# Storing keys and values unsplit, and splitting them in attention

## The chip, the cores and the metric

The kernel runs on one core of a Trainium2 chip. The metric is the device time of one execution in microseconds, as a median of several runs. A core has five engines that run side by side, each from its own queue in order: TensorE (PE in the profile, with PEld for its weight loads), VectorE (DVE), ScalarE (ACT), GpSimd (POOL) and SyncE (SP). SP issues nearly all DMAs of this kernel.

## The reference

One step of a two-layer decoder trunk over 512 prompt rows and 8 x 4 sample rows, 544 rows in all, with 1024 channels. Layer A ends with a projection to shared keys, values and log-forget values; layer B begins with a feed-forward block (FFN) and then attends to them.

```python
def shared_kv(h, kv_norm, w_kvf, b_f, k_norm):
    xs = rmsnorm(h, kv_norm)
    kvf = xs @ w_kvf
    k = rmsnorm(kvf[..., :D_ATT].reshape(bsz, L, N_HEADS, HEAD_DIM), k_norm)
    v = kvf[..., D_ATT:2 * D_ATT].reshape(bsz, L, N_HEADS, HEAD_DIM)
    logf = jax.nn.log_sigmoid((kvf[..., 2 * D_ATT:] + b_f).astype(jnp.float32))
...
# layer B
h = h + 0.5 * swiglu(rmsnorm(h, ffn1_norm[i]), ffn1_w1[i], ffn1_w3[i], ffn1_w2[i])
q = rmsnorm((rmsnorm(h, mix_norm[i]) @ att_w_q[j]).reshape(bsz, L, N_HEADS, HEAD_DIM), q_norm[j])
# per head, for blocks of 128 queries
s = q k^T * scale + csum_q - csum_k          # csum: running sum of logf, causal mask
o = softmax(s) @ v
```

k, v, logf are outputs too. The sample rows attend to pages of a cache in the same way.

## The kernel before

Activations lie transposed: channels on the 128 partitions, the 544 rows on the free axis. Products run in a form of float32 (fp32r) that keeps part of the mantissa, so every factor is split into a high part `hi` (a cast, on ScalarE) and a low part `lo = x - hi` (a subtraction, on VectorE), and a product is three matmuls: hi·hi, hi·lo, lo·hi. `split_pair` (L279, L280) does this for activations, `_split` (L192, L193) for 128x1024 blocks of weights, which stream in by DMA (L159).

SBUF buffers of 4352 bytes a partition are called `big` (44 of them), those of half the size `tmp` (8). PSUM has three buffers `ps` of two banks and two `pb` of one.

The order of each engine's queue is set by the framework's scheduler, which replays the program as written with a model of times and gives every engine a fixed order; only the body of an FFN is in the order of its code. An engine that waits at one instruction holds back everything behind it in its queue.

The places that matter here, in order of time:

- *Projection of shared keys and values* (`kv`). First a tile for the log-forget values, whose further work (`forget`, L801 to L886) runs in the background, on VectorE up to L817, then as a running sum over 512 positions on POOL (nine steps L827) that ends in the cast L836 on ScalarE. Then eight tiles for the heads' keys, then eight for the values, each 48 matmuls into a `ps` buffer. In the values' loop, per head: VectorE scales the value tile (L755); the key of the same head is normalized (`k_norm`, L774), written out, split, and its pair written to `kd` in DRAM; the values of the head before are turned by TensorE (`v_turn`, five transposes L786 and L787 into a `ps` buffer), split from PSUM, their sample rows copied by ScalarE (L791), and the pair written to `vd`. One input of the next FFN is scaled and split (`prep`, L291, L292).
- *Forms for the next FFN.* The FFN multiplies 2x2 blocks by a scheme with seven products, which takes sums and differences of its inputs. `forms` (L301 to L308 and two pairs of splits) makes them for two channel chunks at a time: four sets for the eight chunks. `kv` makes two of them, after heads 3 and 5; `more` in `ffn` makes those that are missing between the four plain tiles at the FFN's start (copied out at L417).
- *FFN body.* The seven products of a block come in the order 1 5 6 2 7 3 4, each into PSUM (L480), with three accumulators in turn, two of them in `ps`. Product 6 goes where 1 was, 7 where 6 was, 4 where 7 was, each after the copy L488 or the sum L497 has emptied it.
- *Attention.* The order of its steps is written by hand in `ORDER`: `f` fetches a head's keys and values, `a` makes its scores, L1011 to L1017 are the softmax, `t` turns the probabilities, `v` multiplies by the values. The scheduler interleaves the steps of neighbouring heads.

Of the kernel before, what the change touches and what calls it, by code (L numbers as in the profile page):

```python
# [22 lines left out]
F32 = mybir.dt.float32  # L23
F32R = mybir.dt.float32r
I32 = mybir.dt.int32
AF = mybir.ActivationFunctionType
ALU = mybir.AluOpType
AX = mybir.AxisListType

P = 128  # L30
D = 1024
NC_ = D // P
SEQ = 512
# [7 lines left out]
NH = 8  # L41
# [42 lines left out]
def whole(p):  # L84

    return p[:].rearrange("p a b -> p (a b)")[:, 512 - CUT:512 - CUT + T]


class Builder:
# [469 lines left out]
    def gmlp(self, h, box, on_chunk):  # L559
# [78 lines left out]
        u_tile(2)  # L638
        assert self.chain is None
        v_turn(0)  # L640
        v_turn(1)
        for c, spatials, turns in ((3, (0,), (2, 3)), (4, (1,), (4,)), (5, (2, 3), (5,)), (6, (4, 5), (6, 7)),
                                   (7, (6, 7), ())):
            u_tile(c)
            for k in turns:
                v_turn(k)
            for k in spatials:
                spatial(k)
# [72 lines left out]
    def kv(self, h, box, ffn_gain):  # L721

        nc, o = self.nc, self.o
        xs = self.pairs(box)
        p, rstd = self.tile_rstd(xs, box["acc"])
        f = self.big()[:, 0, :]
        self.evac(lambda p=p: nc.vector.tensor_tensor(f, whole(p), rstd, ALU.mult))
        self.bg.append(self.forget(f))
        kraw = []
        self.kd = self.dram.tile([NH, P, 2, SEQ], F32, name="kd")  # L730
        self.vd = self.dram.tile([NH, P, 2, SEQ], F32, name="vd")
        self.vsd = self.dram.tile([NS, D], F32, name="vsd")
        sqs, bcs, rows = [], [], {}
        for hh in range(NH):
            p = self.tile_mm(xs)
            if hh % 2 == 0:
                kt = self.big()

            def take(p=p, kc=kt[:, hh % 2, :]):
                nc.vector.tensor_tensor(kc, whole(p), rstd, ALU.mult)  # L740
                kraw.append(kc)
                sqs.append(self.square(kc))
            self.evac(take)
            if hh == 5:
                bcs += self.head_rows(sqs[:4])
            if hh >= 6:
                rows[hh - 6] = bcs[hh - 6]()
        vpend = None
        nxt = {"x": {}, "f": []}
        for hh in range(NH):  # L750
            p = self.tile_mm(xs)
            if hh == 0:
                bcs += self.head_rows(sqs[4:])
            vc = self.tmp()
            last = nc.vector.tensor_tensor(vc, whole(p), rstd, ALU.mult)  # L755
            nc.sync.dma_start(out=o["v"][hh], in_=vc)
            if vpend is not None:
                self.v_turn(*vpend)
            vpend = (hh, vc)
            with self.tc.issue_after(last.ins):  # L760
                self.k_norm(hh, kraw, rows)
            if hh + 2 < NH:
                rows[hh + 2] = bcs[hh + 2]()
            nxt["x"][hh] = self.prep(h[hh], ffn_gain + hh)
            if hh in (3, 5):
                nxt["f"].append(self.forms(h, ffn_gain, len(nxt["f"]), self.pairs(nxt)))
        self.v_turn(*vpend)
        return nxt, rstd

    def k_norm(self, hh, kraw, rows):  # L770
        nc = self.nc
        bc = rows.pop(hh)
        kn = kraw[hh]
        nc.vector.scalar_tensor_tensor(kn, kn, self.gain(G_K), bc, ALU.mult, ALU.mult)  # L774
        nc.sync.dma_start(out=self.o["k"][hh], in_=kn)
        nc.gpsimd.tensor_copy(self.ks[:, hh, :], kn[:, SEQ:])
        pair = self.big(F32R)
        self.split_pair(pair, kn[:, :SEQ], slice(0, SEQ))
        nc.sync.dma_start(out=self.kd[hh], in_=pair[:, :, :SEQ].bitcast(F32))

    def v_turn(self, hh, vc):

        nc = self.nc
        t = self.ps()
        for j in range(4):
            nc.tensor.transpose(t[:, 0, j * P:(j + 1) * P], vc[:, j * P:(j + 1) * P], self.ident)  # L786
        nc.tensor.transpose(t[:NS, 1, :P], vc[:, SEQ:], self.ident)  # L787
        pair = self.big(F32R)
        self.split_pair(pair, t[:, 0, :], slice(0, SEQ))
        vs = self.small.tile([P, P], F32, tag="vs", name=self.name("vs"), bufs=2)  # L790
        nc.scalar.copy(vs[:NS, :P], t[:NS, 1, :P])  # L791
        nc.sync.dma_start(out=self.vd[hh], in_=pair[:, :, :SEQ].bitcast(F32))
        nc.sync.dma_start(out=self.vsd[:, hh * P:(hh + 1) * P], in_=vs[:NS, :P])

    def forget(self, x):
# [173 lines left out]
    def attention(self, xs, acc, h_out, on_chunk):  # L969
        nc = self.nc  # L970
# [3 lines left out]
        st = {}  # L974
        W = (256, 256, 384, 512)

        def fetch(h):
            kp, vp = self.big(F32R), self.big(F32R)
            nc.sync.dma_start(out=kp[:, :, :SEQ].bitcast(F32), in_=self.kd[h])
            nc.sync.dma_start(out=vp[:, :, :SEQ].bitcast(F32), in_=self.vd[h])  # L980
            st["kv", h] = (kp, vp)

        def prep_q(h):
            st["q", h] = self.big(F32R)
# [2 lines left out]
        def qk(h):  # L987
            kp, _ = st["kv", h]
            qp = st.pop(("q", h))
            S = [self.ps(), self.ps()]  # L990
            r0 = 32 * (h % 4)
            for i in range(4):
                out = S[i // 2][:, i % 2, :]
                w, qs = W[i], slice(i * P, (i + 1) * P)
                nc.tensor.matmul(out[:, :w], self.L[r0:r0 + 32, h // 4, qs], self.R[r0:r0 + 32, 0, :w],  # L995
                                 start=True, stop=False)
                nc.tensor.matmul(out[:, :w], qp[:, 0, qs], kp[:, 0, :w], start=False, stop=False)  # L997
                nc.tensor.matmul(out[:, :w], qp[:, 0, qs], kp[:, 1, :w], start=False, stop=False)
                nc.tensor.matmul(out[:, :w], qp[:, 1, qs], kp[:, 0, :w], start=False, stop=False)
                if i == 0:  # L1000
                    nc.tensor.matmul(out[:, :256], self.identr, self.neg[:, 128:384], start=False, stop=True)
                else:
                    nc.tensor.matmul(out[:, (i - 1) * P:(i + 1) * P], self.identr, self.neg[:, 0:256],
                                     start=False, stop=True)
            ps = []
            for i in range(4):
                w = (i + 1) * P
                sc = S[i // 2][:, i % 2, :w]
                m, l = self.sm(1), self.sm(1)
                p = self.tmp()  # L1010
                nc.vector.tensor_reduce(m, sc, AX.X, ALU.max, negate=True)  # L1011
                nc.scalar.activation(p[:, :w], sc, AF.Exp, bias=m, accum_out=l)
                nc.vector.reciprocal(l, l)
                if i in (1, 2):
                    nc.gpsimd.tensor_scalar(p[:, :w], p[:, :w], l, None, ALU.mult)
                else:
                    nc.scalar.activation(p[:, :w], p[:, :w], AF.Copy, scale=l)  # L1017
                ps.append(p)
            st["p", h] = ps
# [17 lines left out]
        def pv(h):  # L1037
            pt = st.pop(("t", h))
            _, vp = st.pop(("kv", h))
            mv = ((pt[0], 0, 512), (pt[1], 0, 384), (pt[2], 0, 256), (pt[2], 256, 256))  # L1040
            acc = self.pb()
            for j, (t3, c0, n) in enumerate(mv):
                vs = slice(j * P, (j + 1) * P)
                out = acc[:, 512 - n:512]
                nc.tensor.matmul(out, vp[:, 0, vs], t3[:, 0, c0:c0 + n], start=j == 0, stop=False)
                nc.tensor.matmul(out, vp[:, 0, vs], t3[:, 1, c0:c0 + n], start=False, stop=False)
                nc.tensor.matmul(out, vp[:, 1, vs], t3[:, 0, c0:c0 + n], start=False, stop=j == 3)
            o[h] = self.big(F32R)
            self.split_pair(o[h], acc, slice(0, SEQ))

# [114 lines left out]
        def project(c):  # L1165
# [5 lines left out]
            on_chunk(c, slice(HT, T))  # L1171

        do = dict(q=tile, s=stat, n=norm, f=fetch, p=prep_q, a=qk, t=turn, v=pv, K=self.load_k, V=self.load_v,
                  z=sample_q, S=sample_qk, T=sample_turn, P=sample_pv, O=sample_out, x=load_vs, h=project_half,
                  o=project)
# [215 lines left out]
```

## Time and profile before

| what | us |
|---|---|
| three runs, median (lowest, highest) | 2083.34 (2082.64, 2084.26) |
| the profiled execution's own time | 2082.28 |
| its span | 2080.5 |
| TensorE busy in the span | 2052.7 |
| VectorE, ScalarE, POOL busy | 1509.0, 940.0, 180.5 |

The span is the time from the first to the last recorded instruction; the execution's own time is 1.8 us longer. In the rows of the profile an instruction is named by line, engine, operation and `out<-in`, and the brackets or the arrow name what ended the idle time ahead of it.

### The profile page before, as it was taken

Reading aid. Unit: us, or ns where it says so; the run is one execution under the profiler, and the core shown is the slowest. Engines: PE = TensorE matmul, PEld = TensorE weight load, DVE = VectorE, ACT = ScalarE, POOL = GpSimd, SP = SyncE. Lnnn points to the kernel's source line nnn. Section 1 sums busy time; section 2 is a strip of 40 time slices with the busy share of each in tenths; the row PEclk is TensorE's granted clock in tenths of the full one; section 3 lists DMA queues with packets and bytes.
Section 4 is the critical chain, followed back from the end, with each engine's and each line's share of the span. In section 5 each row is a group of like instructions: output and inputs, shape, how many; then the busy total and the mean of one; then the engine's idle time right before and its main releaser. Section 6 shows DMA issues by size and latency. Waiting matters only on the chain.

```text
span 2080.5 us, 38809 instructions
## 1 busy us (share of the span) xinstructions
PE 2052.7 (99%) x16388; PEld 2016.0 (97%) x16388; DVE 1509.0 (73%) x1874; ACT 940.0 (45%) x1389; POOL 180.5 (9%) x226
## 2 busy tenths in 40 slices
PE   8999999999999999999999999999999999999999
PEld 8999999999999999999999999999977999999999
DVE  7877777456687878776688777786465797777773
ACT  6534344323554434454355443444364654343451
POOL 0000000300100000052140000002041300000020
PEclk9999999999999999999999999999999999999999
DMA  5223234212223233422193222326467332322321
GB/s 183 90 96 119 72 102 154 83 44 82 86 88 112 78 106 99 136 92 88 62 351 109 99 102 92 112 87 200 150 201 260 102 102 72 112 91 93 126 98 44
DMA packets 93776, 237.94 MB, mean 114 GB/s; under 512 B 9490, under 2 KB 27442, under 8 KB 93602
## 3 DMA queue, kind: packets, MB, share of 16 engines
q1 hardware_dynamic: 93458, 235.42, 33.9%
q8 instruction: 129, 2.11, 0.4%
q14 instruction: 45, 0.37, 0.1%
q10 hardware_dynamic: 144, 0.04, 0.0%
HBM read 218.94 MB, written 16.49 MB: 113 GB/s over the span
## 4 chain that ended last, share of the span: by engine, by line
PE 91%; DVE 4%; ACT 2%; issue 1%; DMA 1%; POOL 1%; SPq 0%; ACTq 0%; DVEq 0%
PE ps L480 32%; PE ps L235 16%; PE ps L241 16%; PE ps L239 16%; PE pb L480 5%; DVE big L193 1%; ACT big L192 1%; PE ps L1149 1%; PE ps L1151 1%; PE ps L1150 1%; DVE big L178 1%; PE ps L997 0%; PE ps L995 0%; PE ps L1110 0%; PE ps L618 0%
## 5 line engine op out<-in xcount | busy, mean ns | idle before, releaser
L480 PE MATMUL ps<-big,big 128*128 128x272 f32 x5616 | 728.4, 288 | 7.5 <-DVE big L497 4.1
L480 PEld LDWEIGHTS ps<-big,big 128*128 128x128 f32 x5616 | 714.3, 188 | 9.0 <-issue 4.7
L193 DVE TENSOR_TENSOR big<-big,big 128x1024 fp32r<-128x1024 f32 (+2 forms) x538 | 590.7, 1100 | 111.8 <-ACT big L192 109.2
L192 ACT CAST big<-big 128x1024 fp32r<-128x1024 f32 (+2 forms) x538 | 486.7, 931 | 269.4 <-DVE big L178 264.1
L235 PE MATMUL ps<-big,big 128*128 128x256 f32 (+1 forms) x2832 | 589.5, 289 | 9.7 <-ACT big L192 7.2
L239 PE MATMUL ps<-big,big 128*128 128x256 f32 (+1 forms) x2832 | 584.3, 287 | 0.0
L241 PE MATMUL ps<-big,big 128*128 128x256 f32 (+1 forms) x2832 | 584.2, 288 | 0.0
L235 PEld LDWEIGHTS ps<-big,big 128*128 128x128 f32 x2832 | 453.8, 189 | 12.9 <-ACT big L192 7.6
L239 PEld LDWEIGHTS ps<-big,big 128*128 128x128 f32 x2832 | 456.4, 189 | 0.0
L241 PEld LDWEIGHTS ps<-big,big 128*128 128x128 f32 x2832 | 453.2, 188 | 1.0 <-DVE big L193 0.5
L320 POOL TENSOR_TENSOR st<-st,tmp 128x544 f32<-128x544 f32 (+1 forms) x63 | 87.4, 1387 | 1601.5 <-ACT tmp L318 1601.2
L519 DVE SCALAR_TENSOR_TENSOR big<-ps,big 128x544 f32<-128x544 f32 x160 | 115.4, 721 | 106.9 <-PE ps L241 106.7
L178 DVE TENSOR_TENSOR big<-big,big 128x1024 f32<-128x1024 f32 x156 | 190.0, 1218 | 0.3 <-DMA big<-in_w 0.3
L488 ACT COPY tmp<-ps 128x544 f32<-128x544 f32 x117 | 71.6, 612 | 138.4 <-PE ps L480 138.4
L443 ACT ACTIVATE big<-big 128x544 f32<-128x544 f32 x88 | 58.0, 661 | 160.3 <-DVE big L440 151.1
L480 PE MATMUL pb<-big,big 128*128 128x272 f32 x936 | 124.0, 288 | 0.0
L440 DVE TENSOR_TENSOR big<-big,st 128x1088 f32<-128x1088 f32 x88 | 112.9, 1289 | 10.1 <-ACT big L502 8.5
L480 PEld LDWEIGHTS pb<-big,big 128*128 128x128 f32 x936 | 120.2, 188 | 0.0
L291 ACT ACTIVATE big<-big,gains 128x544 fp32r<-128x544 f32 (+1 forms) x80 | 56.0, 705 | 123.9 <-DVE big L519 64.9
L280 DVE TENSOR_TENSOR big<-big,big 128x544 fp32r<-128x544 f32 (+1 forms) x104 | 74.4, 721 | 26.1 <-ACT big L279 25.9
L292 DVE SCALAR_TENSOR_TENSOR big<-big,gains,big 128x544 fp32r<-128x544 f32 (+1 forms) x80 | 64.5, 811 | 27.6 <-ACT big L291 27.6
L279 ACT CAST big<-big 128x544 fp32r<-128x544 f32 (+1 forms) x104 | 66.5, 645 | 28.8 <-DVE big L774 15.2
(186 smaller groups left out, 1246.8 us busy)
## 6 DMA issues: line engine op xcount, KB each, us to landing
big<-in_w SPq DMA_DIRECT2D x156, 512.0 KB
big<-in_w2a SPq DMA_DIRECT2D x64, 512.0 KB
big<-in_w2b SPq DMA_DIRECT2D x32, 384.0 KB
big<-in_w13p SPq DMA_DIRECT2D x16, 512.0 KB
big<-in_win SPq DMA_DIRECT2D x16, 512.0 KB
big<-in_wg SPq DMA_DIRECT2D x16, 512.0 KB
big<-in_wkv SPq DMA_DIRECT2D x16, 512.0 KB
big<-in_ck SPq DMA_DIRECT2D x16, 512.0 KB
```

The lines of the kernel that those rows point to most:

```text
L178: self.nc.vector.tensor_tensor(t, a, b, ALU.add if op == "+" else ALU.subtract)
L192: self.nc.scalar.copy(hi, src)
L193: self.nc.vector.tensor_tensor(lo, src, hi.bitcast(F32), ALU.subtract)
L235: i = nc.tensor.matmul(out[:, a:b], wh, xh[:, a:b], start=s, stop=False)
L239: nc.tensor.matmul(out[:, a:b], wh, xl[:, a:b], start=False, stop=False)
L241: nc.tensor.matmul(out[:, a:b], wl, xh[:, a:b], start=False, stop=e)
L280: self.nc.vector.tensor_tensor(pair[:, 1, cols], src, pair[:, 0, cols].bitcast(F32), ALU.subtract)
L320: nc.gpsimd.tensor_tensor(acc[:, cols], acc[:, cols], sq, ALU.add)
L440: tt(g, g, rstd.unsqueeze(1).broadcast_to([P, 2, T]), ALU.mult)
L480: nc.tensor.matmul(dst[w], a[:, c], b, start=k in "152" and kp == 0 and n == 0, stop=kp == NKP - 1 and n == 2, skip_group_check=True)
L488: nc.scalar.copy(t["r" + k], t["C" if k == "5" else "A"])
L519: nc.vector.scalar_tensor_tensor(h[c], whole(out), 0.5, h[c], ALU.mult, ALU.add)
```

## The change

`kd` and `vd`, which held pairs, become one array `kvd` that holds a head's keys and turned values as plain float32. `k_norm` and `v_turn` don't split any more: the normalized key is written straight from where it is, and the turned values are copied out of PSUM once. In attention `fetch` loads both with one DMA and splits them with one cast and one subtraction of 128 x 2 x 512. And `kv` makes three sets of forms rather than two, the third after head 7.

```diff
-        self.kd = self.dram.tile([NH, P, 2, SEQ], F32, name="kd")
-        self.vd = self.dram.tile([NH, P, 2, SEQ], F32, name="vd")
+        self.kvd = self.dram.tile([NH, P, 2, SEQ], F32, name="kvd")
...
-            if hh in (3, 5):
+            if hh in (3, 5, 7):
                 nxt["f"].append(self.forms(h, ffn_gain, len(nxt["f"]), self.pairs(nxt)))
...
         nc.gpsimd.tensor_copy(self.ks[:, hh, :], kn[:, SEQ:])
-        pair = self.big(F32R)
-        self.split_pair(pair, kn[:, :SEQ], slice(0, SEQ))
-        nc.sync.dma_start(out=self.kd[hh], in_=pair[:, :, :SEQ].bitcast(F32))
+        nc.sync.dma_start(out=self.kvd[hh, :, 0, :], in_=kn[:, :SEQ])
...
-        pair = self.big(F32R)
-        self.split_pair(pair, t[:, 0, :], slice(0, SEQ))
+        vt = self.tmp()
+        nc.scalar.copy(vt[:, :SEQ], t[:, 0, :])
...
-        nc.sync.dma_start(out=self.vd[hh], in_=pair[:, :, :SEQ].bitcast(F32))
+        nc.sync.dma_start(out=self.kvd[hh, :, 1, :], in_=vt[:, :SEQ])
...
         def fetch(h):
-            kp, vp = self.big(F32R), self.big(F32R)
-            nc.sync.dma_start(out=kp[:, :, :SEQ].bitcast(F32), in_=self.kd[h])
-            nc.sync.dma_start(out=vp[:, :, :SEQ].bitcast(F32), in_=self.vd[h])
-            st["kv", h] = (kp, vp)
+            raw, hi, lo = self.big(), self.big(F32R), self.big(F32R)
+            nc.sync.dma_start(out=raw[:, :, :SEQ], in_=self.kvd[h])
+            nc.scalar.copy(hi[:, :, :SEQ], raw[:, :, :SEQ])
+            nc.vector.tensor_tensor(lo[:, :, :SEQ], raw[:, :, :SEQ], hi[:, :, :SEQ].bitcast(F32), ALU.subtract)
+            st["kv", h] = [(hi[:, a, :SEQ], lo[:, a, :SEQ]) for a in range(2)]
```

The matmuls of `a` and `v` are the same with the new names. The change also shifts the scheduler's fixed orders. Line numbers of the changed kernel are one or two smaller from L777 on: its L787 is the new copy of the turned values, its L789 the copy L791 of before, its L834 the cast L836, its L813 and L815 the steps L815 and L817, its L978 the new cast in `fetch`.

ScalarE in the values' projection, before, from the second turned head on (`vs` is the sample rows' copy, `ps` a turned head, `gains` marks `prep`):

```order
L279 CAST big_11722<-ps_11716 128x512
L279 CAST big_11732<-big_11121 128x512
L291 ACTIVATE big_11738<-big_87,gains 128x544
L192 CAST big_11741<-big_11573 128x1024
L791 COPY vs_11725<-ps_11716 32x128
L836 CAST tmp_11747<-big_11475 128x512
L279 CAST big_11808<-ps_11802 128x512
L279 CAST big_11818<-big_11121 128x512
L291 ACTIVATE big_11824<-big_87,gains 128x544
L301 ACTIVATE big_11827<-big_86,gains 128x544 x2
L791 COPY vs_11811<-ps_11802 32x128
```

The same place in the changed kernel:

```order
L787 COPY tmp_11714<-ps_11708 128x512
L789 COPY vs_11716<-ps_11708 32x128
L834 CAST tmp_11735<-big_11474 128x512
L787 COPY tmp_11796<-ps_11790 128x512
L789 COPY vs_11798<-ps_11790 32x128
L279 CAST big_11816<-tmp_11814 128x544
L279 CAST big_11817<-tmp_11815 128x544
L192 CAST big_11825<-big_11651 128x1024
```

The two reads of a turned head now follow each other, the keys' splits are gone, and what `prep` did between them stands earlier; the cast of the running sum is still ahead of the third head's copy.

VectorE from the last steps of log-forget to the second head, before (L755 scales a value tile, L774 a key):

```order
L815 SCALAR_TENSOR_TENSOR big_11252<-big_11252 128x544
L817 SCALAR_TENSOR_TENSOR big_10936<-big_11252,big_10936 128x544
L337 SCALAR_TENSOR_TENSOR tmp_11542<-st_11541 128x544
L755 TENSOR_TENSOR tmp_11554<-ps_11482,st_10926 128x544
L774 SCALAR_TENSOR_TENSOR big_11000<-big_11000,gains,tmp_11393 128x544
```

The same steps in the changed kernel:

```order
L337 SCALAR_TENSOR_TENSOR tmp_11541<-st_11540 128x544
L755 TENSOR_TENSOR tmp_11553<-ps_11481,st_10926 128x544
L774 SCALAR_TENSOR_TENSOR big_10999<-big_10999,gains,tmp_11392 128x544
L813 SCALAR_TENSOR_TENSOR big_11251<-big_11251 128x544
L340 SCALAR_TENSOR_TENSOR tmp_11541<-pb_11530,tmp_11541 128x272
L340 SCALAR_TENSOR_TENSOR tmp_11541<-pb_11531,tmp_11541 128x272
L755 TENSOR_TENSOR tmp_11623<-ps_11574,st_10926 128x544
L774 SCALAR_TENSOR_TENSOR big_10999<-big_10999,gains,tmp_11461 128x544
L815 SCALAR_TENSOR_TENSOR big_10936<-big_11251,big_10936 128x544
```

The last step of log-forget, from which POOL's running sum starts, has moved from ahead of the first value tile to behind the second.

ScalarE at the FFN's start, before (L417 copies a plain tile, L301 opens a set of forms, `big<-tmp` casts it, L488 empties product 1):

```order
L417 COPY big_12351<-ps_12358 128x544
L301 ACTIVATE big_12408<-big_88,gains 128x544 x2
L279 CAST big_12413<-tmp_12411 128x544
L279 CAST big_12414<-tmp_12412 128x544
L192 CAST big_12422<-big_12356 128x1024
L417 COPY big_12351<-ps_12428 128x544
L301 ACTIVATE big_12478<-big_89,gains 128x544 x2
L279 CAST big_12483<-tmp_12481 128x544
L279 CAST big_12484<-tmp_12482 128x544
L192 CAST big_12519<-big_12426 128x1024
L192 CAST big_12523<-big_12299 128x1024
```

The same place in the changed kernel:

```order
L417 COPY big_12332<-ps_12339 128x544
L192 CAST big_12389<-big_12337 128x1024
L301 ACTIVATE big_12445<-big_89,gains 128x544 x2
L279 CAST big_12450<-tmp_12448 128x544
L417 COPY big_12332<-ps_12395 128x544
L279 CAST big_12451<-tmp_12449 128x544
L192 CAST big_12486<-big_12393 128x1024
L192 CAST big_12490<-big_12280 128x1024
L488 COPY tmp_12523<-ps_12461 128x544
```

One set of forms is left there, and it starts ahead of the last plain tile's copy.

More of the change, by code (lines that the diff above doesn't have):

```diff
@@ L996, in qk @@
                                  start=True, stop=False)
-                nc.tensor.matmul(out[:, :w], qp[:, 0, qs], kp[:, 0, :w], start=False, stop=False)
-                nc.tensor.matmul(out[:, :w], qp[:, 0, qs], kp[:, 1, :w], start=False, stop=False)
-                nc.tensor.matmul(out[:, :w], qp[:, 1, qs], kp[:, 0, :w], start=False, stop=False)
+                nc.tensor.matmul(out[:, :w], qp[:, 0, qs], kp[0][:, :w], start=False, stop=False)
+                nc.tensor.matmul(out[:, :w], qp[:, 0, qs], kp[1][:, :w], start=False, stop=False)
+                nc.tensor.matmul(out[:, :w], qp[:, 1, qs], kp[0][:, :w], start=False, stop=False)
                 if i == 0:
@@ L1044, in pv @@
                 out = acc[:, 512 - n:512]
-                nc.tensor.matmul(out, vp[:, 0, vs], t3[:, 0, c0:c0 + n], start=j == 0, stop=False)
-                nc.tensor.matmul(out, vp[:, 0, vs], t3[:, 1, c0:c0 + n], start=False, stop=False)
-                nc.tensor.matmul(out, vp[:, 1, vs], t3[:, 0, c0:c0 + n], start=False, stop=j == 3)
+                nc.tensor.matmul(out, vp[0][:, vs], t3[:, 0, c0:c0 + n], start=j == 0, stop=False)
+                nc.tensor.matmul(out, vp[0][:, vs], t3[:, 1, c0:c0 + n], start=False, stop=False)
+                nc.tensor.matmul(out, vp[1][:, vs], t3[:, 0, c0:c0 + n], start=False, stop=j == 3)
             o[h] = self.big(F32R)
```

## The prediction

> **What bounds the kernel now.** I read the page from the top: span, busy shares, then the chain of work that ended last.
>
> ```profile
> span 2080.5 us, 38809 instructions
> PE 2052.7 (99%) x16388; PEld 2016.0 (97%) x16388; DVE 1509.0 (73%) x1874; ACT 940.0 (45%) x1389; POOL 180.5 (9%) x226
> PE 91%; DVE 4%; ACT 2%; issue 1%; DMA 1%; POOL 1%; SPq 0%; ACTq 0%; DVEq 0%
> ```
>
> TensorE is the bound: 2080.5 - 2052.7 = 27.8 us of the span have no matmul in them. The edit adds and removes no matmul, so it can win only out of these 27.8 us, and it can lose only by adding to them. Next I cut the span into stages (columns: stretch, its length, busy time of each engine, clock, DMA share, GB/s).
>
> ```profile
> 1024.00:1081.30 57.30, 54.59 (x444) 52.59 (x442) 52.12 (x75) 27.11 (x46) 29.80 (x32) 1.00 0.79 284
> 1105.40:1130.00 24.60, 21.14 (x164) 20.50 (x163) 21.54 (x25) 15.52 (x20) 0.00 (x0) 1.00 0.26 86
> 1480.00:1600.00 120.00, 118.32 (x957) 94.26 (x956) 70.25 (x159) 63.11 (x155) 28.42 (x58) 1.00 0.72 233
> ```
>
> The first row is the values' projection: PE idles 57.30 - 54.59 = 2.71 us while VectorE is busy for 52.12 of 57.30 us. The second is the start of the next FFN, 3.46 us idle. The third is the head loop of attention, 1.68 us idle. The other 20 us lie at the kernel's ends, in the sample rows at the end of attention and in the other FFNs' starts, which the edit doesn't touch. All that it can win is therefore 2.71 + 3.46 + 1.68 = 7.85 us, 0.38% of the time.
>
> **The values' projection.** The timeline of PE and of ScalarE shows what the 2.71 us wait for (start, duration, in brackets the idle time ahead and its releaser).
>
> ```profile
> 1045.35 0.52 PE L235 MATMUL ps<-big,big 128*128 128x256 f32 x2 [0.76 <-ACT vs L791]
> 1058.46 0.52 PE L235 MATMUL ps<-big,big 128*128 128x256 f32 x2
> 1065.81 0.52 PE L235 MATMUL ps<-big,big 128*128 128x256 f32 x2 [0.56 <-ACT vs L791]
> 1073.14 0.52 PE L235 MATMUL ps<-big,big 128*128 128x256 f32 x2 [0.55 <-ACT vs L791]
> 1080.79 0.63 PE L786 MATMUL ps<-consts,tmp 128*128 128x128 f32 x4 [0.85 <-ACT big L279]
> ...
> 1054.71 0.62 ACT L836 CAST tmp<-big 128x512 fp32r<-128x512 f32 x1 [3.41 <-POOL big L827]
> 1055.24 0.58 ACT L279 CAST big<-ps 128x512 fp32r<-128x512 f32 x1
> 1058.17 0.24 ACT L791 COPY vs<-ps 32x128 f32<-32x128 f32 x1
> ```
>
> A projection tile needs the PSUM buffer of the transposes two tiles back, and that comes free when ScalarE's copy L791 has run. L791 takes 0.24 us, but stands in ScalarE's queue behind the key's split, which waits for VectorE; the last two rows show 2.9 us between the first read of a transposed head and the last one. In the new order the copy of the head and L791 stand side by side, and no VectorE read of PSUM holds the buffer. VectorE loses sixteen subtractions here.
>
> ```profile
> L280 DVE TENSOR_TENSOR big<-big,big 128x512 fp32r<-128x512 f32 x16 | 11.6, 727 | 2.6 <-ACT big L279 2.4
> L280 DVE TENSOR_TENSOR big<-ps,big 128x512 fp32r<-128x512 f32 x16 | 10.9, 683 | 3.5 <-ACT big L279 3.5
> L305 DVE TENSOR_TENSOR tmp<-big 128x544 f32<-128x544 f32 x16 | 12.1, 757 | 12.3 <-ACT big L301 12.2
> ```
>
> Half of each of the first two groups: 8 x 0.727 + 8 x 0.683 = 11.3 us of VectorE gone, against 3.0 us for one set of forms brought in (below). The DMA loses 8 x 0.5 MB of the 57.30 us x 284 GB/s = 16 MB moved here; no PE wait above names a DMA, so I cost that at nothing. SP issues as many DMAs as before, and the queue has slack: each row of norms is issued two heads before its use. So the three L791 waits (0.76 + 0.56 + 0.55 = 1.87 us) go. Of the 0.85 us before the last transposes about 0.5 stays: they need VectorE's product of the last tile (about 0.7 us with its hand-over), and only the previous head's transposes lie between.
>
> What comes instead: the new order moves VectorE's last step of log-forget (L817) behind the second head's products. The running sum on POOL starts from it, and ScalarE's cast L836 waits for that sum in front of the third head's copy.
>
> ```profile
> 1028.78 0.73 DVE L817 SCALAR_TENSOR_TENSOR big<-big,big 128x544 f32<-128x544 f32 x1
> ...
> 1030.45 1.04 POOL L827 TENSOR_TENSOR big<-big 128x512 f32<-128x512 f32 x1
> 1045.36 3.01 POOL L877 TENSOR_SCALAR big<-big,sm 128x256 f32<-128x256 f32 x2 [0.94 <-DVE sm L872]
> ...
> 1029.50:1054.70 25.20, 13.94 (x9) 1.00 0.71 240
> ```
>
> The last row is POOL's nine L827 alone: 13.94 us, 1.55 each, with VectorE busy nearly throughout; the first, with VectorE idle, took 1.04. Two tiles with their transposes run from 1045.35 to 1058.46, 6.55 us each, and without its wait the fourth tile would start at 1044.6; so the second tile ends 6.55 + 0.5 us before, near 1037.5. L817 now follows that tile's product, so with three VectorE steps of 0.7 it ends near 1039.7 instead of 1029.5. Two L827 are done by 1043.2; the third waits behind a copy of the third head's key (about 1045.5) and ends at 1047. Then L877 (2 to 3 us) and six L827: at 1.04 the sum is ready at 1055.3, at 1.55 with 3.0 for L877 at 1059.3. VectorE has some 3 us of two-input work in that stretch of 11, so I take 1057.3. Cast 0.6, copy 0.5, L791 0.25 make 1058.7; the tile that needs this buffer would otherwise start at 1058.46 - 0.76 = 1057.7. New wait: 1.0 us, with ends 0 and 2.9; were all 25.2 us of the chain repeated from 1039.7, it would be 8.5. Behind the blocked ScalarE stand the forms' casts, and VectorE with them, but the tiles that need those have over 4 us in hand. Sum of the stage: -1.87 - 0.35 + 1.0 = -1.2 us.
>
> [...]
>
> **The FFN's start.** Here PE's waits and the work ahead of them are:
>
> ```profile
> 1112.37 3.28 PE L480 MATMUL ps<-big,big 128*128 128x272 f32 x24 [0.87 <-ACT tmp L488]
> 1119.57 6.28 PE L480 MATMUL ps<-big,big 128*128 128x272 f32 x48 [0.90 <-ACT tmp L488]
> 1127.55 2.62 PE L480 MATMUL ps<-big,big 128*128 128x272 f32 x19 [1.70 <-DVE big L497]
> ...
> 1107.40:1110.70 3.30, 3.30 (x28) 3.30 (x27) 2.97 (x5) 2.09 (x3) 0.00 (x0) 1.00 0.58 238
> ...
> PE ps L480 <- DVE big L497: 0.7, 1, 0.7
> ...
> PE ps L480 <- DVE big L497: 1.7, 1, 1.7
> PE ps L480 <- ACT tmp L488: 1.7, 2, 0.9
> ```
>
> The fourth row is the last set of forms: 2.97 us of VectorE in 3.30, right before the FFN's products begin to fill their PSUM buffers. With one set made earlier the last one moves up a tile, and VectorE's run of splits, sums and gates to L497 starts 3 us sooner. L488 then meets its products in time (0.87 + 0.90 go), and L497, 3 us earlier, is late by 0.6 rather than 1.70. The last rows are the same code at two other FFN starts: 0.7 us in all at 570 to 610, where three sets are made ahead, and 1.7 + 1.7 at 1640 to 1720, where none is. So this stage goes from 3.47 to about 0.6: -2.9 us. The set's VectorE and ScalarE work is hidden in the values' projection by the 11.3 us removed there; without that cover it would cost up to 3 us.
>
> **Attention.** Each head now has a cast and a subtraction of 1024 columns, the size of a weight's split.
>
> ```profile
> L193 DVE TENSOR_TENSOR big<-big,big 128x1024 fp32r<-128x1024 f32 x378 | 469.1, 1244 | 82.2 <-ACT big L192 79.9 <-issue 1.9 <-DMA vd<-big 0.2
> L192 ACT CAST big<-big 128x1024 fp32r<-128x1024 f32 x378 | 391.0, 1046 | 269.4 <-DVE big L178 264.1 <-issue 2.5
> 1514.58 0.44 PE L995 MATMUL ps<-big,big 32*128 32x384 f32 x1 [0.70 <-ACT tmp L1012]
> 1510.49 0.16 DVE L1013 RECIPROCAL sm<-sm 128x1 f32<-128x1 f32 x1 [0.53 <-ACT tmp L1012]
> 1546.60 1.34 SPq L979 DMA_DIRECT2D big<-kd  x1
> L997 PE MATMUL ps<-big,big x32: 338/388/504, 1507.6 to 1573.6; 128*128 128x256 f32 x16, 128*128 128x384 f32 x8, 128*128 128x512 f32 x8
> ```
>
> That is 8 x 1.24 = 10.0 us on VectorE and 8 x 1.05 = 8.4 on ScalarE, which are busy 70.25 and 63.11 of 120 us there, so the work fits. The question is what stands behind each pair. Two pairs fall into the first softmax, where PE already waits 0.70 us for an exponential; the subtraction of 1.24 falls on an idle gap of 0.53, so 0.7 us of delay each at the worst, partly made good because two maxima now run back to back. The last head's load was issued at 1546.60, the last scores began before 1573.6, and a load now moves half the bytes; I expect no wait for it. Bounds: nothing hidden, 6 pairs inside the loop x 2.29 = 13.7 us; all waits of the loop gone, -1.7. VectorE's 59% puts it near the lower end: I take +0.5.
>
> **Sum.** -1.2 - 2.9 + 0.5 = -3.6 us. The profiled execution took 2082.28 us, 1.8 around its span, and becomes 2078.7; the median of the runs shown lies 1.06 above it, so I forecast 2083.34 - 3.6 = 2079.7 us. What a measurement of this kernel can tell from no change is about 0.2%, 4.2 us: the forecast is a small gain inside it.
>
> **Rivals.** First, everything falls well: the sum on POOL is ready in time and attention hides its pairs. Then -2.2 - 2.9 + 0 = -5.1 us, 2078.2. For it speak the idle stretches of VectorE in the new order; against it the 25.2 us that this chain took before. Second, POOL runs at the 1.55 us of before: wait 2.9, sum -1.7, 2081.6; at the extreme 8.5, +3.9 and 2087.2. [...] Third, slower: the pairs in attention delay the softmax on which the next scores wait. PE's order there is as tight as the 0.70 us wait shows. If each of the six pairs in the loop exposes its 2.29 us, 13.7 - 4.1 = +9.6 us, 2092.9; it decides from 8.3 us on, when more than half of that is exposed. Against it: VectorE and ScalarE both have idle time beside every head. Fourth, the third set of forms is made early but L497 stays late, since VectorE's queue to it is weights rather than forms: then only 1.77 us go there, 2080.8. The three-set row (0.7) speaks against it.
>
> **Chances.** Forecast with its own spread (2078.6 to 2081) 0.47, a fifth of it beyond 0.2%; first rival 0.25; second 0.13; third 0.08; fourth 0.07. Faster by over 0.2%: 0.25 + 0.10 = 0.35; slower by over 0.2%: 0.08 + 0.01 = 0.09; within: 0.56. The range reaches from the first rival with a full 0.7 us more from attention, 2077.5, to the second, with half of its extreme left out, 2083.
>
> **What would show it.** Right: no L791 wait before the values' tiles; one wait before the sixth of them, released by ScalarE right behind the cast L836 (now two lines earlier), itself waiting for POOL; at the FFN's start no wait on L488 and under 0.8 us on L497; in attention PE idle of 1.5 to 3 us. Wrong: a wait of PE over 3 us in the values' projection, scores waiting for the new cast or subtraction, or an FFN start still above 2 us.

## The result and the profile after

The changed kernel takes 2096.83 us (median of six runs, 2092.47 to 2100.05) against 2084.14 for the kernel before in the same runs: ratio 1.006, 95% interval 1.0048 to 1.0072. It is 13 us slower, where I had forecast 3.6 us less. The page of the profiled execution (2095.62 us) and the stages that the prediction looked at (columns: stretch, its length, busy time of each engine, granted clock of TensorE, DMA share, GB/s):

```profile
span 2093.8 us, 38788 instructions
PE 2061.6 (98%) x16388; PEld 2022.1 (97%) x16388; DVE 1507.5 (72%) x1866; ACT 942.8 (45%) x1389; POOL 179.5 (9%) x226
1024.00:1081.30 57.30, 54.53 (x447) 53.15 (x446) 46.08 (x66) 24.50 (x43) 28.54 (x33) 1.00 0.71 242
1105.40:1130.00 24.60, 23.88 (x190) 23.69 (x190) 21.61 (x24) 15.59 (x20) 0.00 (x0) 1.00 0.29 86
1480.00:1600.00 120.00, 111.81 (x851) 91.69 (x850) 72.24 (x156) 64.11 (x153) 29.51 (x58) 0.91 0.54 173
```

The span grew by 2093.8 - 2080.5 = 13.3 us, and it splits in two. TensorE idles 2093.8 - 2061.6 = 32.2 us instead of 27.8, so 4.4 us are waits: -2.7 at the FFN's start (0.72 left of 3.46), +0.1 in the values' projection (2.77 for 2.71), +6.5 in attention (8.19 for 1.68), the rest elsewhere. The other 2061.6 - 2052.7 = 8.9 us are longer *busy* time for the same 16388 matmuls. The third row shows what goes with it: the granted clock is 0.91 there, and was 1.00 before. At the FFN's start the one wait left is this:

```profile
1123.49 7.75 PE L480 MATMUL ps<-big,big 128*128 128x272 f32 x60 [0.72 <-DVE big L497]
```

Some of TensorE's waits in attention (start, duration, in brackets the idle time ahead and what ended it):

```profile
1507.83 0.33 PE L1026 MATMUL ps<-consts,tmp 128*128 128x128 f32 x1 [0.80 <-ACT tmp L1016]
1508.32 0.38 PE L994 MATMUL ps<-big,big 32*128 32x256 f32 x1 [0.16 <-ACT tmp L1011]
...
1538.16 0.39 PE L997 MATMUL ps<-big,big 128*128 128x256 f32 x1 [0.56 <-DVE big L979]
...
1563.15 0.44 PE L994 MATMUL ps<-big,big 32*128 32x384 f32 x1 [1.84 <-ACT tmp L1011]
...
1569.66 0.80 PE L1044 MATMUL pb<-big,big 128*128 128x512 f32 x1 [2.16 <-ACT big L279]
```

There are ten waits in the stretch, 8.19 us in all, and none names a DMA. Links of the softmax end 3.16 us of them, the splits `split_pair` makes 3.40 us, the output projection's sums (L1160) 1.07 us, and the new subtraction itself (L979) the 0.56 us of the third row. How a pair gets into the softmax's chain, on ScalarE and then on VectorE:

```profile
1555.09 1.03 ACT L978 CAST big<-big 128x1024 fp32r<-128x1024 f32 x1
1556.03 1.05 ACT L192 CAST big<-big 128x1024 fp32r<-128x1024 f32 x1
1556.98 0.68 ACT L1011 ACTIVATE tmp<-ps,sm 128x512 f32<-128x512 f32 x1
...
1555.44 0.67 DVE L1010 TENSOR_REDUCE sm<-ps 128x1 f32<-128x512 f32 x1
1556.16 1.22 DVE L979 TENSOR_TENSOR big<-big,big 128x1024 fp32r<-128x1024 f32 x1
...
1558.80 0.16 DVE L1012 RECIPROCAL sm<-sm 128x1 f32<-128x1 f32 x1
```

The maximum is ready at 1556.11, the exponential starts at 1556.98 behind the pair's cast and a weight's; it ends at 1557.75, and the reciprocal starts at 1558.80 behind the pair's subtraction and a weight's. That is some 1.9 us of delay in one link; how much of it reaches TensorE is not shown by these rows alone.

The same trace cut into stretches of 3.41 us:

```profile
1505.69:1509.10 3.41, 2.46 (x10) 1.49 (x11) 2.43 (x7) 3.17 (x9) 0.47 (x1) 0.99 0.01 2
1509.10:1512.51 3.41, 3.41 (x12) 2.30 (x11) 2.44 (x4) 2.32 (x6) 2.46 (x3) 0.50 0.00 0
...
1515.93:1519.34 3.41, 3.41 (x15) 2.63 (x13) 2.32 (x6) 2.40 (x7) 1.62 (x2) 0.51 0.01 2
1519.34:1522.75 3.41, 3.41 (x16) 2.24 (x15) 1.51 (x6) 2.30 (x8) 0.02 (x1) 1.00 0.00 0
...
1560.30:1563.71 3.41, 1.57 (x9) 1.10 (x9) 0.94 (x4) 1.96 (x6) 0.23 (x1) 0.99 0.81 231
1563.71:1567.13 3.42, 3.42 (x9) 2.31 (x9) 0.00 (x0) 0.32 (x1) 1.10 (x3) 0.50 0.01 4
...
1570.54:1573.95 3.41, 3.14 (x13) 3.14 (x14) 1.27 (x5) 1.40 (x5) 0.49 (x3) 0.51 0.00 0
1573.95:1577.37 3.42, 3.42 (x28) 3.29 (x28) 1.15 (x3) 1.33 (x3) 0.00 (x0) 1.00 0.01 2
```

The clock column reads 1.00 or 0.50 and little between, and it changes on a grid: 1509.1, 1519.3, 1563.7, 1573.9, and once more 1632.0 and 1635.4 are whole numbers of 3.41 us apart. Seven stretches ran at half clock, 24 us in all. Each drop stands right behind a stretch in which TensorE waited: ahead of the first it was busy 2.46 of 3.41 us.

How long a wait is doesn't tell by itself whether a drop follows. The longest of the changed kernel's three stages, 2.40 us in the values' projection, lies across two stretches of that grid (1055.13 to 1061.95, TensorE busy 2.23 and 2.18 of 3.41 us), and the clock stayed at 1.00; 0.80 + 0.16 us of waits in one stretch were followed by the drop at 1509.1.

### The profile page after: what moved, and what is told of

The parts are those of the page before. It is cut to its first block, busy times and chain, and to the rows that moved or that the text cites. A ratio compares the mean times of both kernels' runs of the same rounds, so it can differ in the third digit from the quotient of the medians.

```text
span 2093.8 us, 38788 instructions
## 1 busy us (share of the span) xinstructions
PE 2061.6 (98%) x16388; PEld 2022.1 (97%) x16388; DVE 1507.5 (72%) x1866; ACT 942.8 (45%) x1389; POOL 179.5 (9%) x226
## 4 chain that ended last, share of the span: by engine, by line
PE 91%; DVE 4%; ACT 2%; issue 1%; DMA 1%; POOL 1%; SPq 0%; ACTq 0%; DVEq 0%; POOLq 0%
PE ps L480 32%; PE ps L235 16%; PE ps L241 16%; PE ps L239 16%; PE pb L480 5%; DVE big L193 1%; ACT big L192 1%; PE ps L1148 1%; PE ps L1149 1%; PE ps L1150 1%; DVE big L178 1%; PE ps L994 1%; PE ps L996 1%; PE ps L1109 0%; POOL big L825 0%
## 5 line engine op out<-in xcount | busy, mean ns | idle before, releaser
L235 PEld LDWEIGHTS ps<-big,big 128*128 128x128 f32 x2832 | 453.5, 189 | 12.8 <-ACT big L192 7.1
L488 ACT COPY tmp<-ps 128x544 f32<-128x544 f32 x117 | 71.6, 612 | 138.3 <-PE ps L480 138.3
L280 DVE TENSOR_TENSOR big<-big,big 128x544 fp32r<-128x544 f32 (+1 forms) x96 | 68.3, 719 | 24.1 <-ACT big L279 24.1
L292 DVE SCALAR_TENSOR_TENSOR big<-big,gains,big 128x544 fp32r<-128x544 f32 (+1 forms) x80 | 64.0, 805 | 27.8 <-ACT big L291 27.8
L502 ACT COPY big<-ps 128x544 f32<-128x544 f32 x39 | 24.0, 614 | 105.4 <-PE ps L480 105.4
```

The source lines that it names most:

```text
L235: i = nc.tensor.matmul(out[:, a:b], wh, xh[:, a:b], start=s, stop=False)
L280: self.nc.vector.tensor_tensor(pair[:, 1, cols], src, pair[:, 0, cols].bitcast(F32), ALU.subtract)
L488: nc.scalar.copy(t["r" + k], t["C" if k == "5" else "A"])
```

## The experiments

Labels e1 to e15; times are medians, each ratio is against the kernel before on the same chip.

| run | us | ratio, 95% | PE idle 1480 to 1600 | half-clock windows in the trace |
|---|---|---|---|---|
| before | 2083.34 | 1 | 1.68 | 0 |
| changed | 2096.83 | 1.0048 to 1.0072 | 8.19 | 7 |
| e1 third forms alone | 2080.70 | 0.9977 to 0.9995 | 2.19 | 3 |
| e2 changed, two sets of forms | 2108.02 | 1.0094 to 1.0125 | 9.71 | 12 |
| e3 changed, no splitting in attention | 2080.07 | 0.9972 to 0.9990 | 0.70 | 1 |
| e4 changed, once more | 2096.03 | one run | 8.17 | 7 |
| e5 all fetches 3 steps earlier | 2096.19 | 1.0043 to 1.0069 | 7.16 | 8 |
| e6 heads 0 to 3 earlier | 2104.25 | 1.0084 to 1.0114 | 10.35 | 10 |
| e7 heads 4 to 7 earlier | 2089.31 | 1.0016 to 1.0045 | 4.59 | 6 |
| e8 all 8 steps earlier, cast on POOL | 2099.53 | 1.0066 to 1.0092 | 10.10 | 6 |
| e9 pairs of heads 0 to 3 alone | 2085.04 | 0.9990 to 1.0011 | 0.95 | 5 |
| e10 pairs of heads 4 to 7 alone | 2092.52 | 1.0032 to 1.0058 | 7.64 | 5 |
| e11 values alone unsplit | 2089.43 | 1.0017 to 1.0041 | 3.22 | 3 |
| e12 keys alone unsplit | 2090.57 | 1.0018 to 1.0042 | 6.64 | 6 |
| e13 changed, with 64 filling matmuls | 2110.14 | 1.0111 to 1.0144 | 8.86 (to 1610) | 7 |
| e14 e1 with the same filling | 2093.41 | 1.0030 to 1.0058 | 1.12 (to 1610) | 1 |
| e15 e1, sample rows' split shared | 2079.55 | 0.9973 to 0.9991 | 1.63 | 0 |

The last two columns belong to the one traced execution of each run, which is not always near the median: e1's took 2084.41 us (the slowest of its 11), e2's 2112.55, e3's 2077.96, e7's 2091.88, e8's 2096.32 and e11's 2086.32.

**The parts of the change.** e1 takes the third set of forms alone:

```diff
# on the kernel before
-            if hh in (3, 5):
+            if hh in (3, 5, 7):
```

> The kernel before with only the third set of forms made in the values' projection; keys and values stay stored as pairs. My theory: the FFN's start drops from 3.46 us without a matmul to about 0.7, the values' projection keeps its three waits and gets the set's 3 us of VectorE on top of an already full queue (52.1 of 57.3 us busy), which costs it 0 to 2 us; attention keeps PE's order and its 1.7 us idle, and the granted clock stays 1.00. Time: 0.5 to 2.7 us below before, ratio 0.9987 to 0.9998. The rival, that the third set is itself part of the loss, expects the time above before by several us.

It is faster by 2.6 us in the medians, as expected, and VectorE took the set in the values' projection without the cover that I had said it needed (TensorE idles 2.68 us there). At the FFN's start 1.27 us of waiting were left, rather than 0.7. e2 is the opposite, the changed kernel with `(3, 5)`.

> The changed kernel with two sets of forms, as before the change; keys and values unsplit and split in attention. My theory: the whole loss lies in attention, so this is slower than the changed kernel by the FFN start's 2.7 us: 15 us above before, ratio about 1.007, with 6 to 9 us idle on TensorE in the attention loop and stretches at a granted clock of 0.50. The rival that the third set pushes attention out of step expects a time near before.

It was slower still, 25 us above before, 10 more than I expected: the scheduler made yet another order, with a 3.5 us wait in the values' projection and 12 half-clock windows. So the third set is no part of the loss. e3 takes the splitting out of attention, so that the low parts hold wrong values, and loads twice the bytes, as many as before the change:

```diff
-            raw, hi, lo = self.big(), self.big(F32R), self.big(F32R)
-            nc.sync.dma_start(out=raw[:, :, :SEQ], in_=self.kvd[h])
-            nc.scalar.copy(hi[:, :, :SEQ], raw[:, :, :SEQ])
-            nc.vector.tensor_tensor(lo[:, :, :SEQ], raw[:, :, :SEQ], ...)
+            hi, lo = self.big(F32R), self.big(F32R)
+            nc.sync.dma_start(out=hi[:, :, :SEQ].bitcast(F32), in_=self.kvd[h])
+            nc.sync.dma_start(out=lo[:, :, :SEQ].bitcast(F32), in_=self.kvd[h])
```

> The changed kernel without the splitting in attention: the fetch loads the stored array twice, into the high and into the low tile, as many bytes as before the change, and there is no cast and no subtraction (so the low parts hold wrong values; every other instruction stays). My theory: the sixteen new ACT and DVE instructions, and the order that the scheduler gives TensorE because of them, make the loss. Without them attention has about 1.7 us idle again and a clock of 1.00, and the time is 0 to 3 us below before, ratio 0.9985 to 1.000. The rival that the new place of the stored array or its write and read times make the waits expects about 1.006 still.

2080.07 us, 0.70 us idle in attention: the eight pairs, with the orders that the scheduler makes for them, cause the whole loss, 16.8 us, and the stored array itself none.

```profile
1480.00:1600.00 120.00, 119.30 (x972) 92.60 (x970) 72.70 (x166) 64.09 (x156) 29.29 (x58) 1.00 0.72 240
```

**The clock.** e4 is the changed kernel again.

> The changed kernel once more, for a second trace of the same instructions. In the first trace the granted clock falls to 0.50 at 1509.1, 1563.7 and 1632.0 and is back at 1519.3, 1573.9 and 1635.4: six edges that all lie on a grid of 3.41 us. If the chip judges TensorE's activity in windows of a clock of its own, the waits come out the same here (8 us idle in the attention loop, each within 0.3 us), but the edges lie on a grid with another phase against the program, so that the number of half-clock windows differs (first trace: 7), and the time moves with it by about 1.7 us a window, between 2092 and 2100. If the drops are caused by the program alone, the edges come at the same places within 0.3 us.

The waits came out the same (8.17 us), with seven half-clock windows again. The program ran 0.55 us later and the edges 0.4 us later, so the two traces lay too close in phase to settle anything. What shows that the program alone doesn't fix the drops is e9, below: one list of instructions, 12 runs, from 2078.2 us at a mean granted clock of 1.000 to 2090.4 at 0.993, with 2081.4 at 0.999, 2083.7 at 0.997, 2084.7 to 2085.4 at 0.996 and 2085.3 to 2086.3 at 0.995 in between: 1.7 us for each 0.001. The kernel before does the same on a smaller scale: 2081.9 to 2083.6 in its runs at 1.000, 2087.7 to 2088.3 at 0.997. Only one execution of each run was traced, so that the waits are the same in the others is inferred from e4, not shown.

The traces also show that the longer busy time goes with the half clock. TensorE is busy for 2052.0 us in e15 and 2052.7 before, with no half-clock window, and for 2051.7 in e3 with one; for 2056.1 and 2056.2 with three (e11, e1), 2058.8 and 2058.9 with five (e9, e10), 2061.5 and 2061.6 with seven (e4, the changed kernel) and 2069.6 with twelve (e2): some 1.4 us for each window.

**Is it the place of the pairs?** In e5 every `f` of `ORDER` moves three steps ahead; in e6 and e7 the two halves.

```diff
-q0 K3 K2 K0 q1 q2 q3 K1 s0123 n2 n3 n1 q4 f1 p1 q5 q6 f0 n0 q7 p2 p0 f3 f2 a0 ...
+q0 K3 K2 K0 q1 q2 q3 K1 s0123 n2 f1 n3 n1 q4 f0 p1 q5 q6 n0 q7 f3 f2 p2 p0 a0 ...
```

> The changed kernel with every fetch (its load, cast and subtraction) three steps earlier in the order written by hand; nothing is left out. TensorE's order then is that of before in the first heads and in the last four, save for a few rows. My theory: what costs is the place of the pairs, through the order of TensorE that the scheduler makes of it and through the softmax behind them, not their 18 us of work on ACT and DVE. With the pairs a few us earlier, attention idles 1.5 to 3 us rather than 8.2, at most one stretch of half clock is left there, and the time is 2079 to 2083. The rival, that ACT and DVE simply have no room for 8 x 2.29 us, expects the same sum of waits at other places and 2093 to 2098.

> As the run with all fetches three steps earlier, but for heads 0 to 3 alone; heads 4 to 7 stay where the change has them. By the trace of the changed kernel the waits at 1507 (0.8 us) and 1536 to 1540 belong to the first heads and those at 1554 to 1571 (some 5.5 us with the second half-clock stretch) to the later ones. My theory: the first stretch of half clock (1509 to 1519, some 5 us) mostly goes, the second stays: 2089 to 2093. The rival that the first heads' pairs do all the harm expects 2080 to 2084, the rival that they do none 2095 to 2098.

> The other half: fetches of heads 4 to 7 three steps earlier, heads 0 to 3 where the change has them. My theory: the waits of 1.84 and 2.16 us and the half clock from 1564 to 1574 go (some 8 us together), the wait of 0.8 us and the first stretch of half clock stay: 2086 to 2091. If the first heads' pairs do all the harm, 2095 to 2098.

My theory that the place of the pairs is all that costs fell. e5 gives TensorE nearly the order of before, yet waits 7.16 us, at other places: the first scores now wait 2.5 us for a query's split that stands behind a pair's cast on ScalarE.

```profile
1508.74 0.58 PE L997 MATMUL ps<-big,big 128*128 128x256 f32 x1 [2.55 <-ACT big L280]
...
1506.62 1.03 ACT L979 CAST big<-big 128x1024 fp32r<-128x1024 f32 x1
1507.56 1.66 ACT L280 CAST big<-big 128x512 fp32r<-128x512 f32 x3
```

e6 was even slower than the changed kernel, and only e7 was better, in its expected range. So the place counts for something: wherever the pairs of heads 4 to 7 stay as in the changed kernel (e4, e6 and e10), TensorE waits the same 1.84, 1.89 to 2.16 and 0.96 us late in the loop. In e5 and e7, which move them, these waits are gone and others (1.78 and 1.47 us in e5, 1.48 and 0.90 in e7) have come. e8 moves all fetches eight steps and takes the cast of log-forget's running sum off ScalarE.

```diff
-        nc.scalar.copy(chi[:, :SEQ], cs)
+        pool.tensor_copy(chi[:, :SEQ], cs)
```

> The changed kernel with every fetch eight steps earlier, and with the cast of the running sum of log-forget on POOL instead of ScalarE, so that ScalarE no longer stands at that cast ahead of a turned head. TensorE's order in attention is nearly that of before. My theory: the wait of 2.4 us at the sixth value tile goes and with it nearly all idle time of the values' projection (2.77 to about 0.4 us), the FFN's start keeps its 0.7 us, attention idles 1 to 3 us; with one or no half-clock stretch 2076 to 2081. The rival, that the tiles' buffers are released late for another reason (the copies themselves), keeps 2 us of idle there and gives 2079 to 2083.

Both halves missed. Attention idles 10.1 us. In the values' projection the wait of 2.4 us behind that cast is gone, but TensorE waits 1.32 and 1.39 us there for other work, and the idle time of the stage is 2.71 us as before. The first of the two still comes from POOL: the copy of a turned head itself (L788) waits for log-forget's step L844, which works on `tmp` buffers, as the copy does.

```profile
1064.50 0.58 ACT L788 COPY tmp<-ps 128x512 f32<-128x512 f32 x1 [5.48 <-POOL tmp L844]
```

The second waits for VectorE's scaling of the last value tile (L756).

**How much for how many pairs?** e9 and e10 keep the splitting for one half of the heads; the other half's low parts hold wrong values.

> The changed kernel with the cast and subtraction in attention kept for heads 0 to 3 alone; for heads 4 to 7 the stored array is loaded into the high and the low tile, as in the run without any splitting (so their low parts hold wrong values). That run took 2080.1, the changed kernel 2096.8. Moving the pairs did not help, with TensorE's order like that of before, so my theory now is: a pair in the queues of ACT and DVE delays the softmax or the queries' splits wherever it stands, each such delay of 0.5 to 2.5 us becomes a wait of TensorE, and the waits put windows of 3.41 us below what keeps the clock up, which costs as much again. The two halves then add up. In the changed kernel's trace the first heads have 1 us of waits and the half clock of 1509 to 1519 (5 us): 2084 to 2089 here. The rival that one delay early on puts the whole loop out of step expects 2093 or more here and near 2080 with the last heads' pairs alone.

> The other half: cast and subtraction for heads 4 to 7 alone, heads 0 to 3 loaded without splitting (their low parts hold wrong values). By the changed kernel's trace the later heads have waits of 0.5 + 0.5 + 1.8 + 2.2 + 0.4 us and the half clock from 1564 to 1574: 2086 to 2092. If the halves add, this loss and that of the first heads' run sum to about 16 us over 2080.1.

Over e3, e9 loses 5.0 us and e10 12.4; together 17.4 against 16.8 for all eight pairs. The halves add, within the spread of e9's runs (2078.2 to 2090.4). In e9's trace TensorE waits for only 0.95 us in the whole loop, both waits in one window, and three windows at half clock follow. Of its other two half-clock windows one stands behind the 2.40 us wait of the values' projection, with which the pairs have nothing to do, and one in the output projection, as in e3.

```profile
1510.37 0.33 PE L1031 MATMUL ps<-consts,tmp 128*128 128x128 f32 x1 [0.80 <-ACT tmp L1021]
1510.85 0.38 PE L999 MATMUL ps<-big,big 32*128 32x256 f32 x1 [0.15 <-ACT tmp L1016]
...
1508.29:1511.70 3.41, 2.46 (x10) 1.53 (x10) 2.43 (x7) 3.17 (x9) 0.54 (x1) 0.94 0.01 2
1511.70:1515.11 3.41, 3.41 (x12) 2.30 (x12) 2.25 (x4) 2.25 (x6) 2.40 (x3) 0.50 0.00 0
```

e11 and e12 halve each pair instead: only the values, or only the keys, are stored unsplit and split at the fetch, on top of e1.

> The kernel before with three sets of forms made early and the values alone stored unsplit; the keys stay stored as pairs. Each fetch then brings a cast of 512 columns (0.6 us on ACT) and a subtraction (0.7 on DVE), half of the change's. Values are needed only after the softmax. My theory: half the work gives less than half the loss: 0 to 6 us over the 2080.7 of the run with the third set alone, 2080 to 2087. The rival, that any pair at all upsets the loop, expects 2090 and more.

> The same with the keys alone unsplit and the values stored as pairs. Keys are needed ahead of the scores, so a late cast or subtraction holds up the head itself: my theory expects more loss than for the values alone, 2083 to 2092; no loss at all (2080 to 2082) would say that 0.6 + 0.7 us a head fit, and that it is the length of the pairs that does the harm.

8.7 and 9.9 us over e1 (1.3 of the former in the values' projection, where TensorE idles 4.0 us instead of 2.7): half the work costs about half of the loss, or a little more. The values' projection shifts both numbers: in e12 TensorE idles only 0.86 us there. Less these two differences the values' pairs cost about 7.4 us and the keys' about 11.7, an estimate from medians and one trace each. For the values I had expected at most 6; that they are needed later made them cheaper than the keys, but not free.

**What drops the clock?** I supposed, without a run that shows it, that the scores' narrow matmuls help to bring the drops on. e13 (on the changed kernel) and e14 (on e1) add dense matmuls ahead of each block of scores:

```diff
+                for _ in range(2):
+                    nc.tensor.matmul(out[:, :384], self.identr, self.neg[:, 0:384], start=True, stop=True)
```

> The changed kernel with two matmuls of 384 columns, whose results are overwritten, ahead of each block of scores: 64 in all, at 0.165 us (the 384-column rows stand that far apart) 10.6 us more of TensorE's time. They run when a score's buffer is free, so they fill part of the windows with little streaming, though not the waits themselves. If low streaming is what drops the clock, most of the half-clock time (24 us in the changed kernel's trace, 9 to 10 us of loss) goes and part of the waits is filled: 2092 to 2098, that is 0 to 7 us over the same fill in the kernel with the old order. If the drops don't depend on it, 2103 to 2108.

> The same 64 matmuls in the kernel before with the third set of forms (2080.7 us), for their price: 10.6 us, less what falls into its 0.9 us of waits and its occasional half-clock window (about 1.7 us a run): 2088 to 2091.5 by both theories.

The filling costs 12.7 us on e1 (2 more than its columns) and 13.3 on the changed kernel: nothing was won back, seven windows of e13 still ran at half clock, and both times lie above what I had expected. The filling ran where TensorE had work anyway; the waits stayed, and so did the drops behind them:

```profile
1510.92 0.62 PE L995 MATMUL ps<-neg,identr 128*128 128x384 f32 x2 [1.93 <-ACT tmp L1013]
...
1508.79:1512.20 3.41, 1.49 (x7) 0.91 (x8) 0.90 (x4) 3.38 (x7) 0.97 (x2) 1.00 0.01 2
1512.20:1515.61 3.41, 3.41 (x14) 2.42 (x12) 3.06 (x7) 1.97 (x7) 1.97 (x2) 0.56 0.00 0
```

So filling beside the waits didn't help here, and a wait stands ahead of each drop: cut on their own grids, the traces of the changed kernel and of e1 to e14 show 37 drops between 1440 and 1690, every one right behind a window in which TensorE was busy 0.79 of the time or less. Such a window is no sure sign: 50 of them that ran at full clock in the same stretch were not followed by a drop (1556.89 to 1560.30 of the changed kernel, 2.59 of 3.41 busy, is one).

That the kind of matmul has no part in it is not shown, and the traces speak against it. In the same traces, between 1490 and 1600, in attention, 24 of the 40 full-clock windows that were busy 0.79 or less were followed by a drop, up to 0.78 busy. In the output projection (1600 to 1660), whose matmuls have 272 columns, drops came only behind windows busy 0.50 or less, and at the FFN's start behind it (1660 to 1730) none came, with 42 windows at 0.49 to 0.79. The kernel before has such a window at the earlier FFN's start, half of it idle in one wait of 1.70 us, and the clock stayed:

```profile
1124.27:1127.69 3.42, 1.72 (x14) 1.53 (x13) 3.42 (x5) 0.88 (x2) 0.00 (x0) 1.00 0.00 0
1127.69:1131.10 3.41, 3.41 (x28) 3.41 (x29) 3.41 (x5) 1.51 (x4) 0.00 (x0) 1.00 0.00 0
```

The window of attention ahead of the first drop was busy longer, 2.46 us, but only nine matmuls of 2944 columns began in it; in this one twelve began, of 3264 columns. So a wait was followed by a drop more readily in attention than in a dense stage. What decides over a drop stays open; it isn't the busy time of these rows alone, since the clock stayed behind 1.72 us of 3.42 and fell behind 2.46 of 3.41.

e15 shortens a wait that before, e1 and e3 share, in the output projection:

```diff
# on e1
-                nc.gpsimd.tensor_copy(hi, t[:, :, h, :])
-                nc.gpsimd.tensor_tensor(lo, t[:, :, h, :], hi.bitcast(F32), ALU.subtract)
+                eng = nc.gpsimd if h % 2 == 0 else nc.vector
+                eng.tensor_copy(hi, t[:, :, h, :])
+                eng.tensor_tensor(lo, t[:, :, h, :], hi.bitcast(F32), ALU.subtract)
```

> The kernel before with three sets of forms, and the last sample rows' cast and subtraction (16 small instructions behind one another on POOL, 6 us in the trace, for which TensorE waits 0.6 and 1.8 us) shared between POOL and VectorE. TensorE's order stays. If the half clock follows the waits: these waits fall from 2.4 to 0 to 1 us, the half-clock window behind them (1.7 us a run) mostly goes, the granted clock of most runs is 1.000 rather than 0.999, and the time falls by 2 to 4 us to 2077 to 2079. If it doesn't, the clock stays 0.999 and the time falls by the waits alone, to 2078.5 to 2080.

The three waits became two:

```profile
1613.62 0.39 PE L1150 MATMUL ps<-big,big 128*128 128x272 f32 x1 [1.06 <-DVE big L1162]
1617.45 0.39 PE L1151 MATMUL ps<-big,big 128*128 128x272 f32 x1 [1.82 <-POOL big L1139]
```

Only 0.5 us of waiting went (3.3 to 2.9), less than expected, but 8 of 11 runs now have a clock of 1.000, against 3 of 11 in e1, and the median is 2079.55, 1.2 below e1, though the two ratios' intervals overlap. That is in line with the drop following the waits, though no proof of it. At 0.9982 of the kernel before (0.9973 to 0.9991) it is a little faster than that kernel, and well ahead of the changed one.

## Why the prediction was wrong

- *The FFN's start* was right: -2.7 us against -2.9, and no L488 wait left there.
- *The values' projection*: the three waits of 1.87 us went and about half of the 0.85, as predicted, and the new wait stands where it was predicted, behind the cast L834 that waits for POOL. Its size was 2.40 us, not 1.0, so the stage won nothing. POOL's last six steps took 8.97 us, 1.50 each, so the end that I had worked out with its slower steps, 2.9, was the nearer one. My 1057.3 took VectorE's two-input work as what slows these steps; no run shows that. What the trace shows is three steps of 1.03 to 1.04 us up to 1046.5, with VectorE busy for 2.65 of the 5.75 us from the first one's start, and then the six of 1.50, with VectorE busy for 6.80 of 8.97.

```profile
1058.46 0.62 ACT L834 CAST tmp<-big 128x512 fp32r<-128x512 f32 x1 [13.38 <-POOL big L825]
1058.98 0.58 ACT L787 COPY tmp<-ps 128x512 f32<-128x512 f32 x1
1059.46 0.25 ACT L789 COPY vs<-ps 32x128 f32<-32x128 f32 x1
...
1059.77 0.51 PE L235 MATMUL ps<-big,big 128*128 128x256 f32 x2 [2.40 <-ACT vs L789]
```

- *Attention* is the step that failed. I took +0.5 of bounds -1.7 and +13.7 because VectorE is busy 59% of the loop, an average that says nothing of what a pair of 1.03 and 1.22 us does at the link where it stands. The waits grew by 6.5 us. This is the third rival, to which I gave 0.08, at about half of its full exposure; with the 4.4 us of waits alone the time would have been near 2088, not 2097.
- *A term was missing.* Two thirds of the time lost are no wait at all but TensorE at half clock, 8.9 of 13.3 us in the profiled execution. I read 1.00 in the clock column of before and took it as given. With the measured terms in place of mine the sum is 0.1 - 2.7 + 6.5 + 8.9 = 12.8, of 13.3.
- *What stays open*: why one arrangement of the same eight pairs (e7) ends 9 us above e3 and another (e6) 24. The scheduler makes a new order each time, and no run here held the order fixed while only the pairs' length changed. So how the waits divide between the pairs' own length and the order is not shown. Nor is it shown that the waits alone cause the drops: no run removes a wait of the loop and nothing else.

## What to carry to other kernels

When work is moved onto engines that are half idle, look at the links it will stand in front of, not at the share of busy time: here 2.3 us a head on two engines at 53% and 59% cost 17 us. Where TensorE is the bound, a short wait may cost twice, once for itself and once for half clock behind it: in attention here, a stage of short steps that wait on one another, 0.96 us of waits in one window were followed by three windows at half clock, some 4 us more at the 1.4 us a window above; at this kernel's dense FFN starts waits of up to 1.7 us were followed by none. Read the granted clock in windows of a few us, since on the page's 40 slices the drops don't show (the clock row of the changed kernel is 9 throughout). A spread between runs of one kernel that goes with the mean granted clock, as in e9, is worth a look at the waits.

## What the hardware showed that I had not expected

In attention, less than 1 us of waiting in a window of 3.41 us (0.95 in e9, busy 2.46 of 3.41) was followed by a clock of 0.50, where I had taken the 1.00 of before as given; at an FFN's start 1.70 us was not. Full clock came back after one window of dense matmuls (1632.0 to 1635.4) but after three windows of scores at half clock (1509.1 to 1519.3), and after five in e5 and e6. And the same instructions took 2078.2 us at a mean granted clock of 1.000 and 2090.4 at 0.993 (e9).
